# Building the float32 copy of x with VectorE additions, at a later point, under a planner with shorter matmul durations

## The chip, the cores and the metric

The kernel runs on one core of a Trainium2 chip. The metric is the device time of one execution in microseconds (us), and less is better. Engines are named as in the profile: PE is TensorE (PEld its weight loads), DVE is VectorE, ACT is ScalarE, POOL is GpSimd and SP is SyncE, which here only issues DMAs. POOL also issues some DMAs, in particular all those that add to what already lies in SBUF.

## The reference, cut to what matters

One decoder layer over 512 tokens of width 1024, in float32. It has a gated feed-forward block (FFN) before the mixer and another one after it, both of hidden width 2816:

```python
h = h + 0.5 * swiglu(rmsnorm(h, ffn1_norm), ffn1_wg, ffn1_wu, ffn1_wd)
a = rmsnorm(h, mix_norm); u = a @ w_in          # then two groups of attention heads
h = h + concat[norm(NSA heads), norm(FoX heads)] @ w_out
h = h + 0.5 * swiglu(rmsnorm(h, ffn2_norm), ffn2_wg, ffn2_wu, ffn2_wd)
h = h + sigmoid(norm(h) @ w_g) * norm(p @ w_p)
# swiglu(x, wg, wu, wd) = (silu(x @ wg) * (x @ wu)) @ wd
```

## The kernel before

**Precision.** A float32 operand is held as two fp32r tiles, hi (the rounded value, cast by ACT) and lo (the rest, subtracted by DVE), and a product is three matmuls: hi by hi, hi by lo, lo by hi.

**The FFN.** The 2816 hidden columns are eleven pairs of 128-column blocks. The first pairs ("classic") are ordinary products of the transposed, normed x with the weights, made by `gate_up`: 4 weight tiles of 512 KB, each split into hi and lo, with 24 matmuls of 512 columns each. In FFN1 pairs 0 to 2 are classic, pair 0 being done by `ffn_start` while x arrives; in FFN2 pairs 0 and 1 are. The other pairs are done by class `Blocks` in Strassen's way: 7 products of sums of blocks in place of 8, with 24 matmuls of 256 columns each. These sums need seven operands made from x, and the sums of x blocks are taken in float32, so that x is first put together again from its parts.

**x_operands** (L602) does that. It has four buffers B of the tag `pt` (there are 4 of them), one for each quarter of x. Before the change each is filled by two SP DMAs that copy x's hi part and two POOL DMAs that add x's lo part. In FFN1 each is then multiplied by `row`, the tokens' inverse norms, since in FFN1 the norm is applied late. Then come 4 sums and differences, and 7 splits into hi and lo (operands 7, 5, 6, 1, 4, 2, 3). When B's buffers are done with, the same four `pt` buffers hold the weight sums of `Blocks`, which are an SP load followed by an adding POOL DMA (names `pt<-in_quarters`).

**row** is made by `rms_rows` (L535): ACT squares h for four groups of tokens, POOL turns each sum into an inverse root (`rstd`: a TENSOR_SCALAR and a TENSOR_TENSOR with pow, output `s`), DVE copies it out to 128 columns (`w`), and PE transposes the four copies (`acc<-ident,w`).

**What sets the order.** All instructions are recorded first, with estimated durations (`Plan.cost`, L109) and their dependencies. `Plan.issue` (L212) then emulates the five engines: at each step the instruction that can start earliest on its engine is taken, within a window of 440 recorded instructions behind the oldest that is left. What it takes becomes the order on each engine for good; every engine then works in that order and waits in it. `Plan.weave` (L195) records several streams of the mixer side by side, the one with the least planned PE time first. So the planned durations of matmuls set which instruction stands behind which on all engines, the DMA queues of SP and POOL included.

**The mixer** (`mix`, L1093) projects the normed x in pieces with 24 matmuls each; per piece and token group, ACT, DVE and POOL norm and rotate the heads (`hl` is the result's hi and lo), and PE transposes them (`gub<-ident,hl`) in between the matmuls of the next pieces.

All instructions are emitted at one line, L304, so that the profile tells them apart by tile: `acc` and `gub` are PSUM banks (4 of each), `st` loaded weights, `hi` and `lo` their split, `k` the 128x1024 buffers (the transposed x of FFN1 among them), `x` the larger ones (x's operands among them), `w` buffers of 512 columns.

Of the kernel before, what the change touches and what calls it, by code (L numbers as in the profile page):

```python
# [7 lines left out]
F32 = mybir.dt.float32  # L8
F32R = mybir.dt.float32r
AF = mybir.ActivationFunctionType  # L10
ALU = mybir.AluOpType
# [45 lines left out]
class Plan:  # L57
# [51 lines left out]
    def cost(self, eng, method, a, k, outs, ins):  # L109
        ps = lambda x: x.space == PSUM  # L110
        n = max(self.cols(x) for x in outs[:1] + ins)
        if eng == "tensor":
            f = 4 if method == "matmul" and k["rhs"].dtype == F32 else 1
            m = self.cols(k["lhsT"] if method == "matmul" else ins[0])
            return f * max(m / 1.2 + 2.5, self.cols(outs[0]) / 2.4 + 13.5)
        if eng == "sync":
            b = 4 * n * outs[0].shape[0]
            return max(450.0, b / 360.0)
        if eng == "vector":
            if method in ("tensor_copy", "tensor_scalar", "memset") and not any(ps(x) for x in ins):  # L120
                return 70 + 0.52 * n + 57 * any(hasattr(x, "ap") for x in a[2:4])
            ptr = 57 * any(hasattr(x, "ap") and self.cols(x) == 1 for x in a[2:4])
            return 75 + ptr + (8.0 if method == "reciprocal" else 1.04) * n
        if eng == "scalar":
            extra = 93 * sum(1 for key in ("bias", "accum_out", "scale") if hasattr(k.get(key), "ap")) + 93 * (method == "mul")
            return (52 if any(ps(x) for x in ins) else 94) + 0.833 * n + extra
        if method == "dma_start":
            return 900.0
        if method == "tensor_tensor":
            return 300 + 165 * n if a[-1] == ALU.pow else 130 + 2.1 * n  # L130
        if method == "memset":
            return 130 + 0.75 * n
        return 170 + 3.6 * n if n > 1 else 180.0
# [173 lines left out]
class Layer:  # L307
# [294 lines left out]
    def x_operands(self, xT, row=None):  # L602

        nc = self.nc
        V, G = nc.vector, nc.gpsimd
        B = {}
        for r, c in ((0, 1), (1, 1), (0, 0), (1, 0)):
            b = B[r, c] = self.pt().bitcast(F32)[:, :1024].rearrange("p (k c) -> p k c", k=4)
            cols = slice(256 * c, 256 * c + 256)
            for n in range(2):  # L610
                nc.sync.dma_start(b[:, 2 * n:2 * n + 2], xT[2 * r + n][0].bitcast(F32)[:, :, cols])
            for n in range(2):
                G.dma_start(b[:, 2 * n:2 * n + 2], xT[2 * r + n][1].bitcast(F32)[:, :, cols], accum_op=ALU.add)
            if row is not None:
                V.tensor_mul(b, b, row[:, None, cols].to_broadcast([P, 4, 256]))
        out = {}

        def operand(i, src):
            if i == 3:
                hi, lo = (self.k4((P, 4, 256), F32R) for _ in range(2))  # L620
            else:
                y = self.x8((P, 2, 4, 256))
                hi, lo = y[:, 0], y[:, 1]
            nc.scalar.copy(hi, src)
            V.tensor_sub(lo, src, hi.bitcast(F32))
            out[i] = hi, lo
        t, t3 = self.k4((P, 4, 256)), B[0, 1]
        V.tensor_sub(t, B[0, 0], t3)
        V.tensor_sub(t3, t3, B[1, 1])
        operand(7, t3)  # L630
        operand(5, t)
        V.tensor_add(t, B[1, 1], t)
        operand(6, t)
        operand(1, B[0, 0])
        V.tensor_sub(t, B[1, 0], t)
        operand(4, t)
        operand(2, B[1, 0])
        operand(3, B[1, 1])
        return out
# [32 lines left out]
    def ffn(self, h, xT, quarters, wd, on_token, started=None, row=None):  # L672


        n = FF // (2 * P)
        classic = CLASSIC + (started is not None)
        raw, acts = [], []
        blocks = Blocks(self, range(classic, n), quarters)

        def parts():  # L680
            while raw:
                acts.append(self.hidden_parts(raw.pop(0)))
        X = None
        for p in range(n):
            if p < classic:
                first = p == classic - 1
                if first:
                    blocks.ahead(7, 0, 0)
                products = started if p == 0 and started else self.gate_up(
                    p, xT, quarters, (lambda: blocks.ahead(7, 3, 2)) if first else None)  # L690
                raw.append(self.hidden(products, row))
                if p == 0:
                    X = self.x_operands(xT, row)
            else:
                i = 7 * (p - classic)
                end = i + 7 if p in (3, 7, n - 1) else len(blocks.seq)
                for j in range(7):
                    blocks.ahead(i + j + 7, min(i + j + 5, end), min(i + j + 3, end))
                    if j == 2:
                        parts()  # L700
                    blocks.product(i + j, X)
                raw.append(blocks.acts)
            if p in (3, 7, n - 1):
                parts()
                e = 7 * (p + 1 - classic)
                self.down(h, acts, p + 1 - len(acts), p == n - 1, wd, on_token, lambda: blocks.ahead(e + 7, e + 3, e + 2))
                acts = []
# [858 lines left out]
```

## Time and profile before

| | |
|---|---|
| device time, median of 3 runs | 1120.98 us (1120.34 to 1121.93) |
| device time of the profiled execution | 1120.48 us |
| its span, from the first to the last instruction | 1118.7 us |
| PE busy | 1084.9 us, 97% of the span |
| DVE busy | 759.0 us, 68% |
| ACT busy | 582.4 us, 52% |
| POOL busy | 208.2 us, 19% |
| DMA, mean over the span | 131 GB/s |

PE is the engine to look at: 33.8 us of the span are left when its busy time is taken away, and a change that is not about PE's own work can gain only there, or where PE ran at its lower clock. The other engines matter where PE waits for them. The profiled execution took 1120.48 us, 1.8 us more than its span.

### The profile page before, as it was taken

The numbers are of one execution on the slowest core, as the hardware profiler recorded it, in microseconds if no ns is written. First come the engines' busy times: TensorE is split into PE (matmuls) and PEld (weight loads), VectorE is DVE, ScalarE is ACT, GpSimd is POOL, SyncE is SP. The second block draws the span as 40 slices with busy tenths as digits, with TensorE's granted clock in tenths as the row PEclk, the third lists the DMA queues.
The fourth block names the chain that finished last, engine by engine and source line by source line (L and its number), as shares of the span: only waits on it lengthen the run. The fifth ranks groups of instructions, "written<-read, shape, count | busy, mean of one in ns | idle before, by whom it ended". The sixth has DMA issues, their size and how long they took to land.

```text
span 1118.7 us, 18093 instructions
## 1 busy us (share of the span) xinstructions
PE 1084.9 (97%) x6859; PEld 975.7 (87%) x6859; DVE 759.0 (68%) x1323; ACT 582.4 (52%) x1132; POOL 208.2 (19%) x358
## 2 busy tenths in 40 slices
PE   9799999999999988999999899998999999999998
PEld 7589899988997888988989888887989998899886
DVE  3597358754765687898889785667736874478473
ACT  5345135532543858988788773644523553255351
POOL 4110001000000266443434520411000000000010
PEclk9899999999999999999999999999999999999999
DMA  9677337643434631312012042798724764343431
GB/s 258 177 217 199 104 115 176 189 151 79 148 78 121 208 119 39 76 30 54 21 45 68 33 162 76 209 238 249 207 96 116 185 189 132 97 130 113 140 117 65
DMA packets 88137, 146.13 MB, mean 131 GB/s; under 512 B 14305, under 2 KB 49153, under 8 KB 87793
## 3 DMA queue, kind: packets, MB, share of 16 engines
q1 hardware_dynamic: 78608, 122.86, 33.7%
q0 software_dynamic: 9440, 22.11, 11.6%
q8 instruction: 54, 0.88, 0.3%
q14 instruction: 35, 0.28, 0.1%
HBM read 130.13 MB, written 6.42 MB: 122 GB/s over the span
## 4 chain that ended last, share of the span: by engine, by line
PE 73%; ACT 7%; DVE 6%; POOL 5%; DMA 4%; issue 3%; SPq 2%; POOLq 0%; DVEq 0%; ACTq 0%
PE acc L304 46%; PE gub L304 27%; ACT w L304 2%; POOL s L304 2%; SPq L304 2%; DVE k L304 2%; DVE w L304 2%; ACT k L304 1%; DVE lo L304 1%; DMA pt<-in_quarters 1%; POOL w L304 1%; ACT hi L304 1%; POOL r L304 1%; DMA pt<-k 1%; DVE pt L304 1%
## 5 line engine op out<-in xcount | busy, mean ns | idle before, releaser
L304 PE MATMUL acc<-hi,k 128*128 128x512 f32 (+1 forms) x832 | 263.2, 390 | 3.2 <-DVE k L304 2.2
L304 ACT CAST hi<-st 128x1024 fp32r<-128x1024 f32 (+4 forms) x150 | 148.0, 990 | 191.5 <-PE acc L304 101.5
L304 DVE TENSOR_TENSOR lo<-st,hi 128x1024 fp32r<-128x1024 f32 (+4 forms) x150 | 171.9, 1150 | 91.8 <-ACT hi L304 90.0
L304 PE MATMUL acc<-hi,x 128*128 128x256 f32 (+3 forms) x784 | 204.6, 335 | 0.0
L304 PEld LDWEIGHTS acc<-hi,k 128*128 128x128 f32 x832 | 156.0, 188 | 35.0 <-DVE k L304 2.0
L304 PE MATMUL acc<-lo,k 128*128 128x512 f32 (+1 forms) x432 | 164.6, 384 | 0.0
L304 PE MATMUL gub<-x,hi 128*128 128x256 f32 x816 | 147.6, 282 | 1.7 <-DVE w L304 1.2
L304 ACT CAST hi<-pt 128x1024 fp32r<-128x1024 f32 x68 | 71.2, 1048 | 148.6 <-PE acc L304 88.5
L304 PE MATMUL acc<-x,hi 128*128 128x256 f32 x816 | 147.3, 282 | 0.0
L304 PEld LDWEIGHTS acc<-hi,x 128*128 128x128 f32 x784 | 135.5, 189 | 8.4
L304 DVE TENSOR_TENSOR lo<-pt,hi 128x1024 fp32r<-128x1024 f32 x68 | 83.1, 1223 | 87.8 <-ACT hi L304 87.8
L304 PE MATMUL gub<-k,hi 128*128 128x512 f32 (+1 forms) x560 | 141.4, 343 | 0.0
L304 PE MATMUL acc<-lo,x 128*128 128x256 f32 (+3 forms) x392 | 131.6, 336 | 0.0
L304 PEld LDWEIGHTS gub<-x,hi 128*128 128x128 f32 x816 | 126.1, 189 | 2.6 <-DVE w L304 1.4
L304 PEld LDWEIGHTS acc<-x,hi 128*128 128x128 f32 x816 | 125.6, 188 | 0.0
L304 POOL DMA_DIRECT2D pt<-in_quarters x34 | 29.4, 865 | 477.6 <-DVE w L304 210.7
L304 PE MATMUL acc<-x,lo 128*128 128x256 f32 x408 | 115.4, 283 | 1.4 <-DVE lo L304 1.4
L304 PE MATMUL gub<-x,lo 128*128 128x256 f32 x408 | 115.4, 283 | 0.8 <-DVE lo L304 0.8
L304 PEld LDWEIGHTS gub<-k,hi 128*128 128x128 f32 x560 | 97.6, 192 | 11.4
L304 PE MATMUL gub<-k,lo 128*128 128x512 f32 (+1 forms) x280 | 95.5, 341 | 0.0
L304 PEld LDWEIGHTS acc<-lo,k 128*128 128x128 f32 (+1 forms) x432 | 79.7, 185 | 14.4
L304 PEld LDWEIGHTS acc<-x,lo 128*128 128x128 f32 x408 | 76.9, 188 | 1.8 <-DVE lo L304 1.8
(173 smaller groups left out, 1754.3 us busy)
## 6 DMA issues: line engine op xcount, KB each, us to landing
st<-in_quarters SPq DMA_DIRECT2D x51, 512.0 KB, 3.7
st<-in_ffn_wd SPq DMA_DIRECT2D x44, 512.0 KB, 4.4
pt<-in_quarters SPq DMA_DIRECT2D x34, 512.0 KB, 3.6
pt<-in_quarters POOLq DMA_DIRECT2D x34, 512.0 KB, 6.8
st<-in_quarters SPq DMA_DIRECT2D x32, 256.0 KB, 5.1
st<-in_w_in SPq DMA_DIRECT2D x48, 128.0 KB, 2.6
pt<-k SPq DMA_DIRECT2D x16, 256.0 KB, 3.1
pt<-k POOLq DMA_DIRECT2D x16, 256.0 KB, 9.6
```

Of the source, the lines that this page charges most:

```text
L304: getattr(getattr(self.nc, op.eng), m)(*a, **k)
```

## The change

Two things. In `x_operands` the 16 DMAs that fill B (8 copies on SP's queue, 8 adding ones on POOL's) are replaced by 8 DVE additions of a hi and a lo tile, 128x512 elements each; in FFN1 the call is recorded one pair later (`classic - 2` is pair 1 in FFN1 and pair 0, as before, in FFN2). In `Plan.cost` a matmul is planned shorter: with 128 weight columns, 512 columns go from 226.8 to 215.8 ns, 256 columns from 120.2 to 109.2 ns, and 128 columns stay at 109.2 ns.

```diff
-            return f * max(m / 1.2 + 2.5, self.cols(outs[0]) / 2.4 + 13.5)
+            return f * max(m / 1.2, self.cols(outs[0]) / 2.4) + 2.5
...
     def x_operands(self, xT, row=None):
...
-        V, G = nc.vector, nc.gpsimd
+        V = nc.vector
...
             for n in range(2):
-                nc.sync.dma_start(b[:, 2 * n:2 * n + 2], xT[2 * r + n][0].bitcast(F32)[:, :, cols])
-            for n in range(2):
-                G.dma_start(b[:, 2 * n:2 * n + 2], xT[2 * r + n][1].bitcast(F32)[:, :, cols], accum_op=ALU.add)
+                V.tensor_add(b[:, 2 * n:2 * n + 2], *(y.bitcast(F32)[:, :, cols] for y in xT[2 * r + n]))
...
-                if p == 0:
+                if p == classic - 2:
                     X = self.x_operands(xT, row)
```

POOL's queue at the start of FFN1, before (-) and after (+, none here); `s1_112` to `s1_124` are the four inverse roots of `rms_rows`, `pt_139` to `pt_142` the buffers B, `k4_78` to `k4_84` the lo parts of x:

```order
-L304 DMA pt_139<-k4_78 128x2x256
-L304 DMA pt_139<-k4_80 128x2x256
-L304 DMA pt_140<-k4_82 128x2x256
-L304 DMA pt_141<-k4_78 128x2x256
-L304 DMA pt_141<-k4_80 128x2x256
-L304 DMA pt_142<-k4_82 128x2x256
 L304 ISA
 L304 TENSOR_SCALAR s1_112<-s1_111 128x1
...
-L304 DMA pt_140<-k4_84 128x2x256
 L304 TENSOR_TENSOR s1_120<-s1_120,mhalf_67 128x1
 L304 TENSOR_SCALAR s1_124<-s1_123 128x1
-L304 DMA pt_142<-k4_84 128x2x256
```

Six adding DMAs stood ahead of the four roots and two between their halves; now the roots stand there alone.

DVE in the same place; `pt_160` to `pt_163` are the buffers B now, `lo_141` and `lo_145` the first two weight tiles of pair 1, `k4_84` the lo part of x's last quarter, `w2_113` to `w2_121` copies of the roots:

```order
 L304 SCALAR_TENSOR_TENSOR k4_82<-acc_103,gcol_ffn1_norm_74,k4_81 128x512
+L304 TENSOR_TENSOR pt_161<-k4_81,k4_82 128x512
 L304 TENSOR_TENSOR lo_106<-st_104,hi_105 128x512 x2
+L304 TENSOR_TENSOR pt_162<-k4_77,k4_78 128x512
+L304 TENSOR_TENSOR pt_162<-k4_79,k4_80 128x512
+L304 TENSOR_TENSOR lo_141<-st_139,hi_140 128x1024
+L304 TENSOR_TENSOR lo_145<-st_143,hi_144 128x1024
 L304 SCALAR_TENSOR_TENSOR k4_84<-acc_107,gcol_ffn1_norm_74,k4_83 128x512
 L304 SCALAR_TENSOR_TENSOR k4_84<-acc_108,gcol_ffn1_norm_74,k4_83 128x512
+L304 TENSOR_TENSOR pt_163<-k4_81,k4_82 128x512
 L304 COPY w2_113<-s1_112 128x128
+L304 TENSOR_TENSOR pt_161<-k4_83,k4_84 128x512
```

Though the call is recorded later, the planner puts the additions between the steps of `ffn_start`, and the first weight splits of pair 1 have moved ahead of `k4_84` and of the copies.

PE in the mixer, where the transposes of a piece's heads (`hl_638`) stand between the matmuls of a later piece (`acc_662`), before:

```order
L304 MATMUL acc_662<-hi_612,x8_538 128x256
L304 MATMUL acc_662<-lo_613,x8_538 128x256
L304 MATMUL acc_662<-hi_612,x8_540 128x256
L304 MATMUL gub_639<-ident_66,hl_638 128x128 x2
L304 MATMUL acc_662<-hi_612,x8_538 128x256
L304 MATMUL acc_662<-lo_613,x8_538 128x256
```

And after the change:

```order
L304 MATMUL acc_662<-hi_612,x8_538 128x256
L304 MATMUL acc_662<-lo_613,x8_538 128x256
L304 MATMUL acc_662<-hi_612,x8_540 128x256
L304 MATMUL gub_639<-ident_66,hl_638 128x128 x2
L304 MATMUL acc_662<-hi_615,x8_539 128x256
L304 MATMUL acc_662<-lo_616,x8_539 128x256
```

The transposes come behind 12 of the piece's 24 matmuls instead of behind 6. PE's order within the two FFNs is the same as before.

## Rows read from the trace of the kernel before

**Rows 1.** The page, part 1: PE's busy time, share of the span, instructions.

```profile
PE 1084.9 (97%) x6859; PEld 975.7 (87%) x6859; DVE 759.0 (68%) x1323; ACT 582.4 (52%) x1132; POOL 208.2 (19%) x358
```

**Rows 2.** Busy time by stretch; columns in the first row.

```profile
core 0: us, PE busy (x) PEld busy (x) DVE busy (x) ACT busy (x) POOL busy (x), PEclk, DMA share, GB/s
...
20.00:33.60 13.60, 13.51 (x65) 11.05 (x63) 1.87 (x4) 7.52 (x12) 7.45 (x10) 1.00 1.13 241
33.60:41.90 8.30, 1.10 (x3) 0.54 (x3) 3.40 (x5) 1.05 (x1) 4.64 (x5) 0.70 0.83 180
41.90:47.20 5.30, 5.30 (x14) 4.17 (x14) 2.49 (x4) 3.03 (x5) 0.00 (x0) 0.51 0.86 274
...
60.00:336.00 276.00, 276.00 (x1856) 256.09 (x1855) 180.01 (x204) 113.92 (x139) 13.90 (x16) 1.00 0.53 147
...
380.00:444.00 64.00, 55.67 (x443) 52.66 (x442) 46.20 (x106) 44.02 (x105) 38.19 (x85) 1.00 0.27 80
444.00:640.00 196.00, 192.93 (x1290) 176.19 (x1289) 169.22 (x505) 164.21 (x469) 88.26 (x153) 1.00 0.17 43
640.00:660.00 20.00, 17.46 (x92) 13.94 (x93) 17.13 (x48) 13.92 (x43) 5.83 (x7) 0.91 0.61 221
...
760.00:778.00 18.00, 14.07 (x110) 13.03 (x109) 13.38 (x13) 10.27 (x12) 1.72 (x2) 1.00 0.88 223
778.00:1060.00 282.00, 282.00 (x1915) 262.25 (x1915) 178.92 (x210) 115.30 (x146) 11.93 (x15) 1.00 0.48 140
...
1100.00:1118.70 18.70, 13.63 (x82) 11.92 (x80) 4.47 (x8) 2.32 (x4) 0.00 (x0) 1.00 0.15 53
```

**Rows 3.** Timeline of PE: start, us, instruction, [idle before <- what ended it].

```profile
33.13 0.38 PE L304 MATMUL acc<-ident,w 128*128 128x128 f32 x2
38.34 0.48 PE L304 MATMUL acc<-ident,w 128*128 128x128 f32 x1 [4.83 <-DVE w L304]
41.28 0.70 PE L304 MATMUL acc<-ident,w 128*128 128x128 f32 x2 [2.46 <-DVE w L304]
```

**Rows 4.** Timeline of POOL in the same stretch.

```profile
27.18 0.57 POOL L304 TENSOR_TENSOR s<-s,mhalf 128x1 f32<-128x1 f32 x1
...
28.78 0.23 POOL L304 TENSOR_SCALAR s<-s 128x1 f32<-128x1 f32 x1
36.18 1.24 POOL L304 DMA_DIRECT2D pt<-k  x1 [7.17 <-DMA pt<-k]
36.99 1.04 POOL L304 TENSOR_TENSOR s<-s,mhalf 128x1 f32<-128x1 f32 x1
...
39.20 1.76 POOL L304 TENSOR_TENSOR s<-s,mhalf 128x1 f32<-128x1 f32 x1
```

**Rows 5.** Timeline of SP's queue and ACT: pair 1's first weights.

```profile
12.92 6.61 SPq L304 DMA_DIRECT2D pt<-k  x6
...
19.63 6.39 SPq L304 DMA_DIRECT2D st<-in_quarters  x5
...
28.60 1.05 ACT L304 CAST hi<-st 128x1024 fp32r<-128x1024 f32 x1 [1.18 <-DMA st<-in_quarters]
```

**Rows 6.** Timeline of DVE: operations on two SBUF tiles.

```profile
49.88 1.28 DVE L304 TENSOR_TENSOR k<-w,w 128x512 f32<-128x512 f32 x2
...
51.08 3.49 DVE L304 TENSOR_TENSOR pt<-pt,w 128x1024 f32<-128x1024 f32 x3
```

**Rows 7.** The chain that ended last: start, us, what.

```profile
163.37 2.88 PE gub L304 x24
...
231.91 43.55 PE acc L304 x192
```

**Rows 8.** Timeline around the first block products of FFN2.

```profile
735.79 1.23 DVE L304 TENSOR_TENSOR lo<-st,hi 128x1024 fp32r<-128x1024 f32 x1 [16.38 <-ACT hi L304]
...
762.33 1.05 ACT L304 CAST hi<-pt 128x1024 fp32r<-128x1024 f32 x1 [4.04 <-DMA pt<-in_quarters]
...
776.42 0.51 PE L304 MATMUL gub<-x,hi 128*128 128x256 f32 x2 [1.20 <-DVE w L304]
```

**Rows 9.** PE's waits: who waited for whom, us in total, times, longest.

```profile
PE gub L304 <- DVE hl L304: 7.9, 10, 1.5
```

## Prediction

> **What bounds the kernel now.** I read the busy times first. PE is busy for 97% of the span [rows 1], so only its gaps, and time at its lower clock, can be won by a change that leaves its matmuls alone. Then I cut the span into stretches [rows 2]. The long parts of the FFNs, 60 to 336 and 778 to 1060 us, have no gap at all; the gaps are few and large. There are 7.2 us at 33.6 to 41.9 (8.30 less 1.10), 8.3 us at 380 to 444, 3.1 us at 444 to 640, 2.5 us at 640 to 660, 3.9 us at 760 to 778, and 5.1 us at the end. After the first one PE does not run at full clock: for 5.3 us the granted clock is 0.51, which is 1.2 in place of 2.4 GHz, so the same work at full clock takes 2.7 us, and 2.6 us are lost. Third, I asked who ends the gap at 33.6: the four small transposes of `rms_rows` wait for DVE's copies, 4.83 and 2.46 us [rows 3]. DVE's copies wait for the roots of POOL, and POOL, after the third root's first half at 28.78, stands for 7.17 us in front of an adding DMA `pt<-k`, which may not start until SP's copy into the same buffer has landed [rows 4]. The second half of the root is queued behind that DMA. So PE's first gap is a DMA of `x_operands` in POOL's queue, on which the roots do not depend.
>
> **The change part by part.**
>
> *The 8 adding DMAs of FFN1 leave POOL's queue.* Nothing is left between the roots' halves. The third root's first half already ran at 28.78; its second half takes 0.57 us when nothing is beside it, and the fourth root two such steps (0.23 and 0.57) [rows 4]. All four are done at about 30.2, the copies a few tenths later, and PE asks for them at 33.13 [rows 3]. Slack is 2 to 3 us. The gap goes, and with it the low clock that follows: 7.2 + 2.6 = 9.8 us. What is late next is pair 1's first weight tile. Before, it was issued at 19.63, behind six copies that kept SP's queue from 12.92 on, and was cast at 28.60, 9.0 us after its issue [rows 5]. Now it is issued where those copies stood, near 13, so with the same 9.0 us it is there at 22, the second tile some 3 us later, and PE wants the first at 33.9. But ACT and DVE have the first two splits ahead of x's last quarter now, which PE wants at about 27.7 (24 matmuls of `ffn_start`, 5.4 us, before 33.1). With the second tile at 25 the lo part of that quarter would be ready at about 28.5, and PE would stand for 0.8 us; with the DMAs less crowded, as I expect with sixteen transfers gone from them, not at all. I take 9.8, between 8.0 and 9.8.
>
> By the Trainium skill ("SBUF — State Buffer", on the engines' ports) a DVE operation with two SBUF inputs takes a port from a GpSimd operation that reads SBUF, for the whole instruction; the additions are of that kind, and some of them now stand between the copies. The trace has a root's second half at 0.57 us alone, 1.04 beside a DMA issue, and 1.76 beside that and a DVE subtraction [rows 4], which agrees. If all four took 1.76, the roots would end 4.8 us later, at 35, and the gain would be 1.9 us less.
>
> *The 8 additions on DVE.* Two tiles of 128x512 take 1.28 us [rows 6], 0.64 each, 5.1 us in each FFN. In FFN1 the additions lie where DVE has 1.87 us of work in 13.6 [rows 2], before `row` is there: they cost nothing, and the later place of the call does not matter for them. If that cover were gone they would sit in the stretch up to the first block product. That begins two pairs of 96 matmuls after 33.9, at 226.8 ns each (43.55 / 192, [rows 7]): at 77.4 us. By the new order DVE has 22 operations of 128x1024 at 1.16 (3.49 / 3) and 13 of 128x512 at 0.64 to do in these 43.5 us, 33.9 us; with the additions 39.0. It still fits. I take 0, at worst 3 us if DVE has to wait for PE's products in between as well.
>
> *FFN2.* Here DVE stood idle for 16.38 us up to 735.79, waiting for a weight tile that SP had issued behind the copies [rows 8]. The additions fit there three times over. Everything that follows starts earlier: x's sums, the release of the `pt` buffers, and so the weight sums that are loaded into them. It was one of these, landing at 762.3, that made the first products wait [rows 8]; the gaps sum to 3.9 us [rows 2]. One of them, 1.20 us, is for a DVE result that frees a bank [rows 8], and I let half of that stay. I take 3.4, between 1.5 and 3.9.
>
> *The shorter durations.* They change no matmul, only the order; in both FFNs PE's order is the same. What it is worth is read from the mixer, 380 to 660, where 13.9 us are idle [rows 2], 7.9 of them in ten waits of at most 1.5 us for `hl` [rows 9]. The old durations were PE's real ones: 226.8 ns planned and 226.8 measured at 512 columns, 120.2 and 120.0 (2.88 / 24) at 256 [rows 7]. The new ones are 5 and 9% short. That puts an instruction that waits for other engines behind more matmuls than before: the transposes of `hl_638` behind 6 more, 0.7 us at 120 ns. I expect most of the `hl` waits to go, since they are no longer than a few matmuls, and some new ones elsewhere, as DVE is busy for 169 of 196 us between 444 and 640. Bounds: all 13.9 us gone, or as much again added. I take a gain of 5, nearest to the row for `hl` less three given back.
>
> By the Trainium skill ("TensorE: Matmul & The Clock Gate", on the gap between matmuls) matmuls at full clock follow each other at the columns divided by 2.4 GHz plus about 2.5 ns, 215.7 ns for 512 columns, which is the new formula. This trace has 226.8 ns, 5% more; so here the old numbers were the right ones.
>
> **The sum.** 9.8 + 0 + 3.4 + 5 = 18.2 us. The profiled execution's span becomes 1100.5, with the 1.8 us around it 1102.3; the median of the runs shown lies 0.5 us above the profiled run, so I say 1103.
>
> **The rivals.**
> 1. *The mixer gives nothing, or loses up to 6 us.* For it: the plan's PE is now faster than the real one, so DVE and ACT may stand in front of a product that is not there yet, with weight splits queued behind. Against it: the FFNs' order hardly changes, and PE's own waiting instructions all moved back. Sum: 13.2 less 0 to 6: 1108 to 1114.
> 2. *Another operand is late at the first gap, or DVE is the bound before FFN1's first product*, 1 to 4 us lost of the 9.8: 1104 to 1107. For it: DVE is busy for all of 12.8 us after the gap in the kernel before. Against it: the sums above leave 2 and 10 us of slack.
> 3. *Slower.* In 380 to 444 PE has 8.3 us of gaps and a full clock; after the gaps at 33.6 (7.2 us in 8.3) the clock was at 0.51, and between 640 and 660 (2.5 us in 20) it was 0.91. If the new order doubled the gaps in 380 to 444 (8.3 us) and they drew together so that a quarter of the 55.7 us of matmuls ran at 1.2 GHz (13.9 us), the mixer would lose 22 us against 13.2 won: 1130. It decides from a loss of 13.2 us on.
> 4. *The mixer loses all its gaps*, 13.9 instead of 5 us: 1094. This is what the page's 215.7 ns would bring if it held here, the plan being exact then. Against it: the measured 226.8.
>
> That the change does not do what it says can be left out: the adding DMAs are gone from POOL's queue.
>
> **How the numbers follow.** The forecast has 0.63 (its own range is 1097 to 1108), rival 1 0.19, rival 2 0.08, rival 3 0.05, rival 4 0.05. Below 1096 lie rival 4 and a little of the forecast, above 1112 rival 3 and a third of rival 1: some 0.17 left out, so the range is 1096 to 1112. What a measurement here can tell from no change is about 0.2%, 2.2 us. Faster: all but rival 3 and a sliver of rival 1, 0.93; same 0.02; slower 0.05.
>
> **What would show it.** In the profile after: the transposes of `rms_rows` without a wait, no PE gap near 33 to 42, a full clock there, and the first product of FFN1 near 77 us; no adding DMA before the first weight sums in POOL's queue; the FFN2 stretch after its second pair with less than 0.5 us of gaps; PE's wait for `hl` well below 7.9 us. I am wrong if a gap of over 2 us stays before 42 us, if FFN1's first product waits, or if the mixer from 380 to 660 us takes longer than before.

## The result and the profile after

The kernel after takes 1096.2 us (median of 4 runs, 1096.0 to 1097.4) against 1121.0 of before on the same chip: a ratio of 0.978, with a 95% interval of 0.9763 to 0.9797. That is 24.8 us less; the prediction was 1103, 18.2 us less than the profiled run, with a range of 1096 to 1112. So the time lies at the very edge of the range, 7 us from the forecast and outside the 1097 to 1108 that the prediction gave for its own sum. The profiled run of after is the longest of its four: 1097.4 us, with a span of 1095.5.

The page, part 1, of after, answering to [rows 1] (PE's busy time, share of the span, instructions):

```profile
PE 1076.8 (98%) x6859; PEld 973.8 (89%) x6859; DVE 769.2 (70%) x1339; ACT 579.6 (53%) x1132; POOL 197.7 (18%) x342
```

PE has 18.7 us of idle time where it had 33.8, and its busy time is 8.1 us shorter with the same 6859 matmuls: the low clock after the first gap is gone, and so are rows of matmuls that are longer beside a wait (an example follows below). To see where the 23.2 us of span come from, I cut both traces at the same four instructions: FFN1's first block product, the mixer's first 288-column matmul, the first matmul of FFN2, and FFN2's first block product. Busy time by stretch, before (start and end, length, busy time and instructions of PE, granted clock, DMA share, GB/s):

```profile
0.00:87.99 87.99, 79.04 (x335) 0.94 0.80 216
87.99:373.82 285.83, 284.12 (x1902) 1.00 0.50 142
373.82:716.33 342.51, 328.38 (x2147) 1.00 0.25 75
716.33:759.85 43.52, 43.52 (x193) 1.00 1.00 256
759.85:1118.70 358.85, 349.84 (x2289) 1.00 0.47 139
```

The same five stretches, after:

```profile
0.00:78.29 78.29, 76.08 (x336) 1.00 0.64 186
78.29:361.75 283.46, 283.46 (x1901) 1.00 0.51 144
361.75:698.60 336.85, 325.01 (x2147) 1.00 0.25 74
698.60:742.12 43.52, 43.52 (x193) 1.00 0.77 217
742.12:1095.50 353.38, 348.77 (x2289) 1.00 0.46 135
```

The differences are 9.7 us in the start, 2.4 in FFN1, 5.7 in the mixer, none in FFN2's first two pairs, and 5.5 behind FFN2's first product. The prediction had 9.8, nothing, 5, nothing and 3.4. Together that is 5.1 us more than forecast, most of it in FFN1 and in FFN2. The rest of the 7 us is the median, which it put 0.5 us above the profiled run and which lies 1.3 us below it.

The start, answering to [rows 3, 4]. PE's timeline after:

```profile
33.94 0.77 PE L304 MATMUL acc<-ident,w 128*128 128x128 f32 x5
34.64 0.73 PE L304 MATMUL gub<-k,hi 128*128 128x512 f32 x2
```

And POOL's, where only the roots are left:

```profile
25.75 1.03 POOL L304 TENSOR_TENSOR s<-s,mhalf 128x1 f32<-128x1 f32 x1
...
28.45 0.88 POOL L304 TENSOR_TENSOR s<-s,mhalf 128x1 f32<-128x1 f32 x1
...
29.72 0.55 POOL L304 TENSOR_TENSOR s<-s,mhalf 128x1 f32<-128x1 f32 x1
```

The last root ends at 30.27, so the transposes start 3.7 us later, find their copies ready, and the next product follows without a gap. PE's waits after, answering to [rows 9]:

```profile
PE gub L304 <- DVE hl L304: 7.0, 8, 1.5
```

Here the prediction expected "well below 7.9". The wait is almost what it was, although the mixer is 5.7 us shorter.

FFN2's first products, answering to [rows 2, 8]: the additions' eight rows on DVE, and PE in two stretches of 18 us:

```profile
702.05 4.90 DVE L304 TENSOR_TENSOR pt<-k,k 128x512 f32<-128x512 f32 x8
```

```profile
742.00:760.00 18.00, 18.00 (x152) 1.00 0.75 199
760.00:778.00 18.00, 18.00 (x154) 1.00 0.68 176
```

The additions run at 0.61 us each, 40 us ahead of the first product, and PE has no gap. What follows them is early too: SP issues the first weight sum's load 17.7 us after FFN2's first matmul (716.27 less 698.60), where it was 28.5 us (744.85 less 716.33). Before, then after:

```profile
744.85 0.33 SPq L304 DMA_DIRECT2D pt<-in_quarters  x1
```

```profile
716.27 0.33 SPq L304 DMA_DIRECT2D pt<-in_quarters  x1
```

In the kernel before, a matmul just behind a wait has a longer row than its like a little later, 0.39 against 0.28 us, so the price of a wait is more than its idle time:

```profile
772.34 0.39 PE L304 MATMUL acc<-x,lo 128*128 128x256 f32 x1 [0.89 <-DVE lo L304]
...
772.80 0.28 PE L304 MATMUL acc<-x,lo 128*128 128x256 f32 x1
```

### The profile page after: what moved, and what is told of

Its sections match the earlier page's. It is cut to its first block, busy times and chain, and to the rows that moved or that the text cites. A ratio compares the mean times of both kernels' runs of the same rounds, so it can differ in the third digit from the quotient of the medians.

```text
span 1095.5 us, 18060 instructions
## 1 busy us (share of the span) xinstructions
PE 1076.8 (98%) x6859; PEld 973.8 (89%) x6859; DVE 769.2 (70%) x1339; ACT 579.6 (53%) x1132; POOL 197.7 (18%) x342
## 4 chain that ended last, share of the span: by engine, by line
PE 88%; POOL 4%; DVE 3%; ACT 2%; issue 2%; DMA 0%; POOLq 0%; ACTq 0%; DVEq 0%
PE acc L304 54%; PE gub L304 34%; POOL s L304 2%; POOL w L304 1%; DVE w L304 1%; ACT w L304 1%; DVE k L304 1%; POOL r L304 1%; DVE lo L304 1%; ACT k L304 1%; ACT hi L304 1%; DVE s L304 0%; DMA ident<-in_ident 0%; DVE pt L304 0%; ACT pt L304 0%
## 5 line engine op out<-in xcount | busy, mean ns | idle before, releaser
L304 PEld LDWEIGHTS acc<-lo,x 128*128 128x128 f32 x392 | 74.0, 189 | 4.4
```

The lines of the kernel that those rows point to most:

```text
L304: getattr(getattr(self.nc, op.eng), m)(*a, **k)
```

## The experiments

Each kernel was timed in five rounds beside the kernel before. Where a length of a stretch is given, it is between the four instructions named above.

**Additions alone.** The kernel after with the old durations:

```diff
-            return f * max(m / 1.2, self.cols(outs[0]) / 2.4) + 2.5
+            return f * max(m / 1.2 + 2.5, self.cols(outs[0]) / 2.4 + 13.5)
```

> The additions in their later place, with the old matmul durations. PE's order is then that of the kernel before throughout. From the two profiles the change's 23.2 us of span lie in five places: 9.7 up to FFN1's first block product, 2.4 at FFN1's end, 5.7 in the mixer, 5.1 in FFN2's first products, 0.4 behind. Theory A (each edit has its own place): the start and FFN2 come from the additions, the mixer from the durations; 14.8 us gained, 1106, and 1104 if FFN1's end goes with the additions. Rival B (what the mixer gains comes from transfers and queues that the additions relieve, and the shorter durations do nothing): 22 to 25 gained, 1096 to 1099. In the profile A has the mixer's PE waits for hl and its gaps as in the kernel before.

Measured: 1105.1 us, ratio 0.986 (0.9838 to 0.9881). The five stretches:

```profile
0.00:76.67 76.67, 74.33 (x335) 1.00 0.66 191
76.67:363.45 286.78, 284.10 (x1902) 1.00 0.51 142
363.45:706.12 342.67, 328.58 (x2147) 1.00 0.25 74
706.12:749.64 43.52, 43.52 (x193) 1.00 0.81 217
749.64:1103.00 353.36, 348.68 (x2289) 1.00 0.46 134
```

The start and the last stretch have all of their gain, the mixer and FFN1 have none: theory A, and FFN1's end does not go with the additions.

**Durations alone.** The kernel before with the diff's first hunk only.

> The kernel before with the shorter matmul durations alone; the sixteen copies and sixteen adding DMAs stay. PE's order is that of the kernel after throughout. Theory A: the mixer's 5.7 us alone, 1115, or 1113 if FFN1's end goes with the durations; the gap at 33.6 and the low clock behind it stay, FFN2's first products keep their 3.9 us. Rival B: nothing, 1121, within 1 us.

Measured: 1110.1 us, ratio 0.9906 (0.9887 to 0.9925), more than either theory said. FFN1 takes 283.95 us and the mixer 337.61, so both of these gains are the durations'; the last stretch stays at 358.67. The rest of the gain is in the start, which I did not expect to move:

```profile
0.00:83.43 83.43, 76.33 (x336) 0.96 0.83 225
...
367.38:704.99 337.61, 326.14 (x2148) 0.99 0.25 75
```

POOL's timeline there:

```profile
31.22 1.25 POOL L304 DMA_DIRECT2D pt<-k  x1 [2.32 <-DMA pt<-k]
...
35.07 1.24 POOL L304 DMA_DIRECT2D pt<-k  x1 [1.69 <-DMA pt<-k]
```

The new durations put SP's last two copies behind four weight transfers instead of five; SP issued them at 22.96 instead of 26.12, and POOL's wait of 7.17 us [rows 4] became 2.32 and 1.69. So the two edits overlap: the 4.6 us won here are part of what the additions win anyway. 16.5 of the one and 11.5 of the other less 4.6 are 23.4, near the measured 24.8. How much of the 4.6 is SP's order is not exact, since with the adding DMAs in place the start varies by up to 3.2 us between kernels that leave it alone (last experiment).

**The adding DMAs behind the roots.** The kernel before, told only that FFN1's adding DMAs come after the `rms` row:

```diff
...
+            nc.after = () if row is None else [self.rooted]
             for n in range(2):
                 G.dma_start(b[:, 2 * n:2 * n + 2], ..., accum_op=ALU.add)
+            nc.after = ()
```

> The kernel before, old durations, all sixteen copies and adding DMAs kept; only the planner is told that FFN1's adding DMAs come after the rms row is done, so that in POOL's queue all eight stand behind the last root. Theory A (the gap at 33.6 is the queue, not the transfers): the gap of 7.2 us and the low clock of 2.6 us go, 9 to 10 gained, 1111 to 1112, with as many bytes moved as before. Rival C (the copies and adding DMAs crowd the first weight and x transfers, or the additions' speed matters): the gap shrinks by less than half, 1117 to 1121. If FFN1's end gains too, 1109.

Measured: 1112.5 us, ratio 0.9925 (0.9906 to 0.9944). The start, and POOL's timeline in it:

```profile
0.00:76.61 76.61, 74.92 (x335) 1.00 0.87 240
```

```profile
25.87 0.55 POOL L304 TENSOR_TENSOR s<-s,mhalf 128x1 f32<-128x1 f32 x1
...
26.91 0.55 POOL L304 TENSOR_TENSOR s<-s,mhalf 128x1 f32<-128x1 f32 x1
27.45 9.98 POOL L304 DMA_DIRECT2D pt<-k  x8
```

All transfers are still there, and more bytes per second move than in the start of before, but the gap and the low clock are gone. The gap was POOL's queue and not the transfers. The start wins 11.4 us; 3.3 are given back in FFN1 (289.08 us), partly among the first products, one of which waits 1.21 us for DVE, whose sums of x come later now, and partly at FFN1's end.

**Additions in FFN1 alone.** As the first experiment, but with copies and adding DMAs kept where `row is None`.

> Additions in FFN1 alone; FFN2 keeps its copies and adding DMAs; old durations. Theory A: the start's 9.7 us, 1111, and 1109 if FFN1's end goes with FFN1's additions; FFN2's first products keep 3.9 us of gaps and 5.1 us to lose, so the run lies 5 us above the one with additions in both. Rival D (FFN2's gap goes because the whole kernel comes earlier or because FFN1's buffers were freed earlier): FFN2's gap is gone here too, and the two runs are alike within 1 us.

Measured: 1110.9 us, ratio 0.9912 (0.9891 to 0.9933), 5.9 us above the run with additions in both FFNs. The last stretch:

```profile
749.26:1108.10 358.84, 349.75 (x2289) 1.00 0.49 139
```

It is 5.5 us longer than with FFN2's additions, and PE's waits are nearly those of before (1.4, 1.2, 1.0 and 0.8 us, there 1.4, 1.2, 0.5 and 0.8). FFN2's gain is FFN2's additions; rival D falls. By which path they give it is not separated: the weight sums are loaded earlier, but the copies and adding DMAs are also gone from the transfers (DMA share 1.00 in FFN2's first two pairs before, 0.77 after), and no run kept these transfers in FFN2 and changed their place alone.

**The early call.** The kernel after with `if p == 0` in place of `if p == classic - 2`.

> The kernel after, with the call of x_operands back behind FFN1's first pair; additions and shorter durations stay. The additions then stand ahead of pair 1's weight splits on DVE where they can, 0.64 us each. Theory A (the additions lie where DVE has time, the place of the call is worth nothing): 1096, within 1.5 us of the kernel after. Rival E (the later place is needed, since additions ahead of the row or the splits make PE wait): 1099 to 1106, with PE waits for DVE between 30 and 90 us in the trace.

Measured: 1096.4 us, ratio 0.9773 (0.9758 to 0.9789): as after. The later place is worth nothing, and DVE's additions cost nothing in either place.

**Shorter, longer, and shorter still.** The kernel after with other durations, 0.95 and 0.90 times the new ones and 1.05 times the old:

```diff
-            return f * max(m / 1.2, self.cols(outs[0]) / 2.4) + 2.5
+            return 0.95 * (f * max(m / 1.2, self.cols(outs[0]) / 2.4) + 2.5)
```

> The kernel after with all of the planner's TensorE durations times 0.95 (205 for 512 columns, 104 for 256). The mixer took 342.5 us of the span by the old durations and 336.9 by the new. Theory F (a shorter planned matmul puts the waiting PE instructions behind more matmuls, so margin grows): the mixer gains again or stays, 333 to 337 us, 1093 to 1096 in all. Rival G (any other table only deals the order anew, and this one was a lucky deal): the mixer anywhere from 336 to 345, 1096 to 1105.

> The kernel after with the old durations times 1.05 (238 for 512 columns, 126 for 256), so longer than the measured ones. Theory F (margin): the mixer loses, 344 to 349 us against 342.5 by the old durations, 1107 to 1112 in all, with more PE waits for hl than the ten by the old. Rival G (a new deal each time): the mixer anywhere from 336 to 345, 1098 to 1108.

> The kernel after with TensorE's durations times 0.90 (194 for 512 columns, 98 for 256). The mixer took 351.7, 342.5, 336.9 and 332.0 us of the span with 238, 227, 216 and 205 for 512 columns. Theory F (margin): a further gain, smaller since 10 us of idle time are left there: 327 to 332, 1086 to 1091. Rival L (at some point PE's plan runs so far ahead of DVE and ACT that they get their work in the wrong order): 333 to 340, 1092 to 1099.

Measured: 1090.9 us at 0.95, ratio 0.9727 (0.971 to 0.9743); 1117.1 at 1.05 times the old, ratio 0.9963 (0.995 to 0.9977); 1094.6 at 0.90, ratio 0.9768 (0.9752 to 0.9784). The mixer in the longer, the 0.95 and the 0.90 kernel:

```profile
366.24:717.94 351.70, 335.71 (x2148) 0.99 0.25 73
```

```profile
359.77:691.74 331.97, 321.69 (x2148) 1.00 0.26 75
```

```profile
360.24:694.85 334.61, 325.07 (x2148) 0.99 0.25 75
```

With 238, 227, 216 and 205 ns for 512 columns the mixer takes 351.7, 342.5, 336.9 and 332.0 us: no scatter, as rival G wanted, but a slope, as F said. The slope is steeper than F had it: both mixers and both totals, of the longer and of the 0.95 kernel, lie outside F's ranges. At 194 it stops, and the total lies where rival L had it. But L's reason is not what the trace shows: PE's idle time is less again (9.5 us, 10.3 at 205), and what grew is busy time, by 3.4 us. About 3 us of that are lost at the lower clock in two stretches, which the 205 kernel does not have:

```profile
425.24:430.24 5.00, 4.13 (x23) 0.66 0.01 3
...
620.24:625.24 5.00, 4.57 (x20) 0.66 0.98 389
```

It is not one unlucky run: the granted clock of the whole run is 0.995 to 0.998 in the four runs at 194 and 0.999 to 1.000 in the four at 205. With the time lost at the lower clock taken off in each, an estimate from stretches of 5 us, the five mixers are about 349, 341, 337, 332 and 331 to 332 us: a slope that becomes flat. The 0.95 kernel beats both kernels.

In that kernel PE's wait for `hl` is smaller; at 0.90 it is all but gone, and others have come in its place (first the 0.95 kernel, then the 0.90 one):

```profile
PE gub L304 <- DVE hl L304: 4.6, 6, 1.1
PE gub L304 <- ACT k L304: 1.3, 1, 1.3
```

```profile
PE gub L304 <- ACT k L304: 1.8, 3, 1.0
...
PE gub L304 <- DVE hl L304: 0.4, 1, 0.4
```

In the longer kernel theory F expected more of these waits than the ten by the old durations. There are fewer, and the mixer is 9.2 us longer all the same:

```profile
PE gub L304 <- DVE hl L304: 6.7, 7, 2.0
```

So the slope does not follow the waits for `hl`.

**The interleaving by the old durations.** `weave` adds up planned PE time, so new durations also change which stream is recorded next. Here it goes by the old ones, and `issue` by the new:

```diff
-            self.pe += op.cost
...
+            self.pe += f_ * max(m_ / 1.2 + 2.5, self.cols(outs[0]) / 2.4 + 13.5)
```

> The kernel after, but the interleaving of the mixer's streams (weave, which adds up PE's planned time) goes by the old durations; issue alone has the new ones. Theory F1 (the gain is in the issue order: PE's waiting instructions stand behind more matmuls): the mixer takes 336 to 338 us as in the kernel after, 1095 to 1097.5. Theory F2 (the gain is the other interleaving of the streams): 341 to 344 us, 1100 to 1103.

Measured: 1094.0 us, ratio 0.9762 (0.9746 to 0.9779), a little below F1's range, the mixer 336.01 us. The profiled run is the longest of its four (1096.7 us). The interleaving is not the cause; the old one does no worse than the new.

**Every result later for PE.** Old durations, but DVE's, ACT's and GpSimd's results are planned to reach PE 400 ns later:

```diff
-           "vector": dict(tensor=255.0, scalar=128.0, ...),
+           "vector": dict(tensor=655.0, scalar=128.0, ...),
```

> Additions in their later place and the old matmul durations, but every result of DVE, ACT and GpSimd is planned to reach TensorE 400 ns later (655, 660 and 550 ns in place of 255, 260 and 150). That gives PE's waiting instructions margin without touching a duration or the interleaving of the streams. Theory F1 (margin in the issue order): the mixer gains 3 to 8 us against the 342.7 of the run with the additions alone, 1097 to 1102. Theory F2 (it is the interleaving): 341 to 344, 1104 to 1106.

Measured: 1106.1 us, ratio 0.9865 (0.985 to 0.9879). The mixer:

```profile
363.77:707.24 343.47, 327.65 (x2147) 1.00 0.25 73
```

No gain. The number is that of F2, but the run before this one has excluded the interleaving; and F1 falls in the form of a fixed margin ahead of each of PE's waiting instructions. What is left open is said below.

**FFN1's end, first try.** In the kernel before DVE stands 5.61 us for a small load at FFN1's end:

```profile
335.44 0.20 DVE L304 TENSOR_SCALAR gf<-gf 128x64 f32<-128x64 f32 x1 [5.61 <-DMA gf<-in_q_norm_fox]
```

So I put that scaling and `gq`'s on GpSimd in the kernel before:

```diff
...
-        nc.vector.tensor_scalar(self.gf[:, 0], self.gf[:, 0], 0.125, None, op0=ALU.mult)
+        nc.gpsimd.tensor_scalar(self.gf[:, 0], self.gf[:, 0], 0.125, None, op0=ALU.mult)
```

> The kernel before; the two scalings of gf and gq in mix_consts (128x64) are on GpSimd, where nothing waits behind them; no other instruction moves on any engine. In the kernel before DVE stood 5.6 us for gf's load at FFN1's end, and the durations alone took 1.9 to 2.4 us off FFN1. Theory H (that is DVE's queue behind gf): PE's gaps at 340 to 345 go, 2 to 2.5 us gained, 1118.5 to 1119.5. Rival I (PE is late there for the last weight tiles, whose issues SP has behind the small loads): less than 0.7 us gained, 1120.5 to 1121.5.

Measured: 1121.6 us, ratio 1.0005 (0.9992 to 1.0018). DVE's wait for `gf` is gone (it stands 6.76 us for ACT instead) and nothing is won: theory H falls, and no gain is what rival I had. ACT's and PE's timelines show what was behind it:

```profile
341.09 1.05 ACT L304 CAST hi<-st 128x1024 fp32r<-128x1024 f32 x1 [7.99 <-DMA st<-in_ffn_wd]
```

```profile
344.86 0.50 PE L304 MATMUL acc<-hi,k 128*128 128x512 f32 x1 [3.35 <-ACT k L304]
```

ACT waits for a weight tile that SP issued after the small loads. The profiled run is 2.2 us above the median of its kernel, and its gap of 3.35 us at PE is 0.57 us in the kernel before, so the size of these two waits may be that run's alone. The longest wait in the place was a wait without a price.

**FFN1's end, second try.** The same kernel, and the small loads planned behind FFN1's last weight load:

```diff
+        nc.after = [self.last_load]
         self.cos, self.sin = c("cos", (P, NT, 16)), c("sin", (P, NT, 16))
         ...
+        nc.after = ()
```

> The kernel before, with mix_consts' small loads planned behind FFN1's last weight load, so that SP issues the four last ffn_wd tiles ahead of them, and with the two scalings of gf and gq on GpSimd as in the run in which that alone gave nothing. PE and ACT keep their order. In that run ACT stood 8.0 us for an ffn_wd tile that SP had issued behind the small loads, and PE 3.4 us at FFN1's last products. Theory I (FFN1's end is SP's order): those gaps go, FFN1 from its first block product to the first 288-column product takes 283 to 284 us as in the kernel after, 1118.5 to 1119.5. Rival K (the last weight tiles wait for a free buffer or for the DMA engines, not for SP): no gain, 1120.5 to 1122.

Measured: 1117.2 us, ratio 0.9966 (0.9953 to 0.9979). FFN1:

```profile
84.76:367.99 283.23, 283.23 (x1902) 1.00 0.52 144
```

No idle time is left and FFN1 is as short as after, 2.6 us less than before: theory I, although the time came out below its range. By the medians 3.8 us were won, 1.2 more than FFN1 gives. The profiled run is the shortest of its nine, 2.2 us below their median, and its start is short too (84.76 us against 87.99), where this edit moves nothing: with the adding DMAs in place, the start took 87.99, 87.13 and 84.76 us in three kernels with the same order of POOL's queue there. Why it varies was not looked into.

## Why the prediction was right, and where it was not

- **The gap at 33.6: right in cause and size.** 9.8 us were forecast, 9.7 came. The queue was shown to be the cause by the run that kept every transfer. In the other runs with the additions the start is 76.5 to 76.9 us, so the profiled run of after is 1.5 us long there, and the gain is up to 11.3. The roots beside DVE's additions take 0.88 and 1.03 us where the last, alone, takes 0.55. DVE made the last copy at 30.5, 3.4 us ahead of the transposes, and that slack hid it. By the Trainium skill ("SBUF — State Buffer", on the engines' ports) a DVE operation with two SBUF inputs and a GpSimd operation that reads SBUF take turns at a port. The rows agree in kind.
- **The additions on DVE: right.** Zero was taken, and the runs with the call in either place agree within 0.3 us.
- **FFN2: the mechanism right as far as it was tested, the term too small.** 3.4 was forecast within 1.5 to 3.9, and 5.5 came. Two things were missing. I let half of the 1.20 us for DVE's bank stay, and all of it went: 4.4 us of idle time are gone, 3.9 there and 0.5 at the kernel's end. And I summed idle time alone, while rows of matmuls beside a wait are longer and count as busy (0.39 us against 0.28 above): PE's busy time in this stretch fell by 1.07 us with the same 2289 instructions, at full clock both times.
- **The mixer: the size right by luck, the mechanism not.** 5 was forecast and 5.7 came, and the durations are the cause, since the two runs with one edit each separate them. But "I expect most of the `hl` waits to go" failed: 7.0 of 7.9 us stayed, and the 5 was taken from them. Idle time fell by 2.3 us in all (14.1 to 11.8), of which `hl` is 0.9 and the rest are small waits for ACT and DVE. Busy time fell by 3.4 us, nearly half of it the low clock at the mixer's end (1.6 us, 0.09 of 17.46 [rows 2]; after, the granted clock is 1.00 there). That part is luck of the profiled run: with the same order on PE the durations alone and the early call met the low clock there, and their mixers take 337.6 and 337.7 us. So the durations give 4.8 to 4.9 us that come again. The slope over four tables speaks against a merely lucky order, and the run with the old interleaving shows that the gain comes from the order of issue. Why a plan with PE 5 to 14% too fast is better, and a plan with late results for PE is not, stays open. One difference can be named: a duration that is short runs up over a stretch of matmuls, a latency does not. No run tested that.
- **FFN1's end: a term that was not there.** The prediction set FFN1 at nothing because "in both FFNs PE's order is the same". The step that failed is that it looked at PE's queue only. The durations also moved SP's queue: an `ffn_wd` tile now stands between the small loads instead of behind them, and 2.4 us went with it.
- **The rivals.** Rival 4 named 1094, near the result, and yet it did not happen: 11.8 us of the mixer's idle time are there. Its reason was the Trainium skill's 215.7 ns between 512-column matmuls ("TensorE: Matmul & The Clock Gate", on the back-to-back gap). After the change 192 matmuls take 43.52 us, 226.7 ns each, as before, so the new plan is not exact, and one that is further off is better still. Rivals 1 to 3 did not come.

## What to carry to other kernels

A DMA that must wait in a computing engine's queue costs what is queued behind it: moving such DMAs behind short work that others wait for can win as much as removing them (here 11.4 us in the start, though 3.3 came back behind it). When a planner's numbers change, compare every queue, the one that issues the loads above all, and not only the busiest engine's; and tune such numbers by measured time, since the true durations need not give the best order. The longest wait in a place may have no price; take it away alone before it is believed.

## What the hardware showed

The same instructions can meet the lower clock or not. At the mixer's end after and the run with the durations alone have the same order on PE and nearly the same gaps (0.92 and 1.40 us, and 0.90 and 1.40). After, in two stretches of 5 us there:

```profile
622.27:627.27 5.00, 2.68 (x19) 1.00 0.32 92
627.27:632.27 5.00, 4.78 (x27) 1.00 1.02 387
```

And with the durations alone, in the 5 us behind the second gap:

```profile
632.38:637.38 5.00, 5.00 (x19) 0.66 0.99 359
```

The granted clock fell to a mean of 0.66 (part of the time at 1.2 in place of 2.4 GHz), which is 1.7 us of lost work (0.34 of 5.00); after, it stayed at 2.4 GHz. The run with the early call has 0.66 in 5 us there too. A difference of this size in one place says nothing about an edit.
